# Four spots reordered in a two-layer float32 backbone: early partial sums, fold low parts on GpSimd, one weight split and one operand split moved

## The chip, the core and the metric

The kernel runs on one core of a Trainium2 chip. The metric is the device time of one execution in microseconds; the time of a kernel is the median of several runs. TensorE (PE) does the matmuls, VectorE (DVE), ScalarE (ACT) and GpSimd (POOL) do the elementwise work, and most DMAs are issued from the queue of SyncE (SP), a few from ACT's.

## What is computed

The reference runs two layers over 1024 latent tokens of width 1024 in float32, and a last RMSNorm. The even layer is a convolution branch and a bidirectional RG-LRU branch behind one input and one output projection; the odd layer is a pooling mixer. Cut to what the change touches:

```python
def even_mixer(h, h0, p):
    z = h @ p["w_in"]
    va, vg, ga, xb, gb = jnp.split(z, ...)
    y_a = conformer_conv(va, vg, p) * jax.nn.silu(ga)
    y_b, hT = rglru_branch(xb, p, h0, True)
    y_b = y_b * jax.nn.silu(gb)
    return jnp.concatenate([y_a, y_b], axis=-1) @ p["w_out"], hT

def odd_mixer(h, p, on_grid):
    u, g = jnp.split(h @ p["w_in"], [W_POOL], axis=-1)
    d = multiscale_pool(u) ...                       # four groups
    y = jnp.einsum("bngi,gij->bngj", d, p["w_grp"]) * p["scale"]
    return (y * jax.nn.silu(g)) @ p["w_out"]

for l in range(2):
    x = x + gate * mixer(modulate(rmsnorm(x)))
return rmsnorm(x, final_g)
```

## The kernel before

**Numbers in two parts.** A float32 matmul is done as three matmuls in a rounded format: every operand is split into a high part (a cast on ACT) and a low part (source minus high part, a subtraction, on DVE or POOL), and high by high, high by low and low by high are added up in PSUM. In names, `h` and `l` are the parts: `wh_gb` and `wl_gb` of a raw weight `wr_gb`, `y_b22h` and `y_b22l` of an operand. A low part needs its cast, and the cast needs the load.

**Quads.** The output projections of both layers, and more, work on quads: a 2 by 2 block product done as seven half-sized products by a Strassen-like scheme. The operand blocks are called `b11, t1, t2, b21, t3, b22, t4`; each product is 12 matmuls of 128x512. Three PSUM tiles, `qa`, `qc`, `qb`, hold the sums; `put` takes one out (DVE, `scalar_tensor_tensor`, PSUM times a gate plus what was there) before the next product that reuses or continues the tile may write it. A quad's weights are two loads `wr_...`, three sums of them, and seven splits into `wq_..._1` to `_7` (`wquad_steps`).

**Four places matter here**, in the order of the program.

- *gb products* (lines 1216 to 1250). The gate projection of the LRU branch, product by product of 48 matmuls, while DVE runs the convolution and `gated(n)` forms `sb = yr * sb`, its cast `ybh` (ACT) and its low part `ybl` (POOL); `yr` is loaded back from DRAM through a small ring of buffers. `gb_weights(j)` loads and splits the weight of product j: load on SP, cast `wh_gb` on ACT, low part `wl_gb` on POOL. `gb_silu(j)` reads product j out (`sb`, ACT). On ACT, POOL and DVE these steps run in the order in which the code is written (`act`, `cast`, `gp`, `vec` chain each instruction behind the one before on its engine). The weights `gb_weights(8)` and `(9)` are those of the next products, `wob`.
- *woa* (lines 1530 to 1600): the other half of the even layer's output projection, four quads of two row blocks each. `put` adds a product onto `x1`, which is first loaded from `x1_part` (the input plus the LRU half, stored at line 1260). The load sits in `put`, just ahead of the add, on SP. In the last quad `woa_ahead` also loads the four weights of fold 2 (`wr_wu_2_0` to `_3`), which the fold products after the last quad use; the low parts of the first two are made on DVE, those of the others on POOL. `square_acc` squares each finished block on ACT (`n1q`) and adds it up on DVE (`n1acc`).
- *wo1* (lines 1960 to 2035): the second part of the odd layer's output projection. Two quads are interleaved: `q0.b11, q0.t1, ..., q0.b21, q2.b11, q0.t3, q0.b22, q2.t1, q0.t4, ...`. Between `q0.b21` and `q2.b11` stands the block that loads operand t3, the weights of quad 2 (`wo1_weights(1, 2)`), the operands b22 and t4, and two blocks of `x2`.
- The operands of wo1 come from DRAM (`y_b22`, `y_t4`, two tiles of 128x1024 each) into rotating pools, b22 into one pool, t4 into another (`y_operands`, line 1790).

**What sets the order.** Within one engine the instructions run in program order. A scheduler writes that order when the kernel is built, from the code's order, the ties `issue_after` and `high_priority`, and the time at which it expects a tile's buffer to come free. So a step can end up elsewhere than where it is written.

Of the kernel before, what the change touches and what calls it, by code (L numbers as in the profile page):

```python
# [20 lines left out]
KT = D // P  # L21
H = 512
HALF = (slice(0, H), slice(H, S))
# [28 lines left out]
def body(ctx, tc, xT, ctxT, cc, ccol, modT, modW, win, gw, wout, wu, grp, wg, wo1, small, edge, ident, outT):  # L52
# [44 lines left out]
    def split(src, hi, lo, eng):  # L97
        return (nc.scalar.copy(hi, src),  # L98
                eng.tensor_tensor(out=lo, in0=src, in1=hi.bitcast(F32), op=sub))

    def held(after):
        return tc.issue_after(after.ins) if after is not None else nullcontext()
# [974 lines left out]
    def vtile(name):  # L1077
        return vpool.tile([P, H], F32, tag="v", name=name)
# [157 lines left out]
    gb_product(5, gws[5])  # L1236
    gated(1, 3)
    for j in range(3, KT + 1):
        if j == 4:
            gb_weights(j + 2)  # L1240
        if j < KT:
            gb_silu(j)
        if 4 < j < KT - 1:
            gb_weights(j + 2)
        if 3 < j < KT - 2:
            gb_product(j + 2, gws[j + 2])
        gated(j - 1, (0, 0, 4, 5, 5, 3, 1, 0)[j - 1])
        if j == KT:
            gb_weights(KT + 1)
            fill(8)  # L1250
        ln_sums()
# [239 lines left out]
    def quad_linked(w, name, ops, put, ahead, order, pend, other):  # L1491
# [35 lines left out]
                put(1, 0, b, None)  # L1527
        return nxt_, (last if len(order) == 2 else (lambda: run("t3"), last))

    def woa(m, w, ahead, pend):  # L1530
        for q in range(2):
            x1[m + q] = xtile(f"x1_{m + q}")

        def put(i, h, x, part):
            v, dr = x1[m + i][:, HALF[h]], x1_part[m + i][:, HALF[h]]
            if part != 1:
                nc.sync.dma_start(v, dr)
            nc.vector.scalar_tensor_tensor(out=v, in0=x, scalar=m0[:, 0, 2 * KT + m + i : 2 * KT + m + i + 1],
                                           in1=v, op0=mult, op1=add)
            if part != 0:  # L1540
                if m < KT - 4 or (m == KT - 4 and (i, h) == (0, 0)):
                    nc.sync.dma_start(dr, v)
                else:
                    late.append((dr, v))
                    if wlate:
                        late_stores()
                square_acc(nacc[h][:, :H], v, (m, i) == (0, 0), f"n1q{m}_{i}_{h}")
        return quad_linked(w, f"woa{m}", ya, put, ahead, {0: ("b22",), KT - 2: ("t3", "b22")}.get(m, ("b22", "t3")),
                           pend, m % 4 == 2)
# [10 lines left out]
    def w_raw(g, kp, out, eng=nc.gpsimd, low=None):  # L1560
        raw = wpool.tile([P, D], F32, tag="wr", name=f"wr_wu_{g}_{kp}")
        d = nc.sync.dma_start(raw, wu[g, kp])
        if out is None:
            hi, lo = [wpool.tile([P, D], F32R, tag=v, name=f"{v}_wu_{g}_{kp}") for v in ("wh", "wl")]
        else:
            hi, lo = [out(f"{v}_wu_{g}_{kp}", F32R) for v in ("wh", "wl")]
        split_held(raw, hi, lo, eng, low)
        return d, (hi, lo)

    def woa_ahead(m):  # L1570
        w = wo_weights(m + 2) if m < KT - 2 else None
        for _ in range((0, 4, 2, 0)[m // 2]):
            next(mods)
        if m == KT - 4:
            sel2.append(hpool.tile([P, H], F32R, tag="cH", name="sel2"))
            selector(sel2[0], nc.gpsimd)
        if m == KT - 2:
            with ExitStack() as octx:
                for v in parted:
                    octx.enter_context(tc.issue_after(v.ins))  # L1580
                g2.append(fold_in(2, d2tile, d2tile))
                octx.enter_context(tc.issue_after(graws[2].ins))
                for kp in range(2):
                    d, w_ = w_raw(2, kp, W2[kp], nc.vector)
                    w2.append(w_)
            wlate.append(d)
            late_stores()
        return w

    sel2 = []  # L1590
    last_ = None
    for m in range(0, KT, 2):
        w0, last_ = woa(m, w0, lambda: woa_ahead(m), last_)
    last_()
# [193 lines left out]
    def y_operands(part, raws, names=BOPS, alloc=None, later=None, hold=None):  # L1788
        for name in names:
            y_operand(yops[part], part, name, next(raws),  # L1790
                      alloc or (dtile if name in ("b11", "b21", "t4") else d2tile), later, hold)
# [11 lines left out]
    def wo1_weights(part, m, mid=None):  # L1803
        return wquad([wo1[m + i, part] for i in range(2)], f"wo{part}_{m}", wo1_ring,
                     part == 1 and m >= KT - 4, mid=mid)
# [204 lines left out]
    with tc.issue_after(q0.evac.ins):  # L2010
        late_ = []
        y_operands(1, iter([None]), BOPS[4:5])
        with held(y_loaded[0]):
            w = wo1_weights(1, 2)
        with tc.issue_after(loaded[0].ins):
            y_operands(1, iter([None] * 2), BOPS[5:], later=late_)
        for v in late_:
            split(*v, nc.vector)
        with held(y_loaded[1]):
            x2_load(2)  # L2020
# [313 lines left out]
```

## Time and profile before

| what | value |
|---|---|
| time, median of 3 runs | 1267.16 us (1267.01 to 1267.77) |
| span of the profiled execution, first to last instruction | 1263.6 us |
| outside the span, median less span | 3.56 us |
| granted TensorE clock, mean | 0.998 |
| busy: PE, DVE, ACT, POOL | 1249.8, 1139.3, 653.8, 295.7 us |

The profile is of one execution, and no time beside its span is recorded for it, so the median stands for its own time. PE is busy for 99% of the span. Timeline rows give the start and the length in us, the engine, the line, the operation with output and inputs, the count, and in brackets the idle time before it with what ended it. A matmul of 128x512 lasts 0.39 us, but the next starts 0.227 us after it, so gaps between starts show a wait. Line numbers are those of the kernel before; in the changed kernel they are 7 to 14 higher behind the second spot.

### The profile page before, as it was taken

How to read it: one execution, taken by the hardware profiler on the slowest of the kernel's cores; microseconds unless marked ns; L12 is line 12 of the kernel's file. 1: busy time of each engine (PE TensorE's matmuls, PEld its weight loads, DVE VectorE, ACT ScalarE, POOL GpSimd, SP SyncE). 2: the span in 40 equal slices, each digit the busy share in tenths (PEclk: the TensorE clock that was granted, in tenths of full speed). 3: DMA queues.
4: the chain of work that ended last, by engine and by line, in shares of the span. 5: the costliest groups of instructions: out<-in, count | busy, mean ns of one | idle time of the engine just before them, and what ended most of it. 6: DMA issues, size and time to landing. Idle time of an engine off the chain costs nothing.

```text
span 1263.6 us, 16209 instructions
## 1 busy us (share of the span) xinstructions
PE 1249.8 (99%) x5866; PEld 1035.6 (82%) x5866; DVE 1139.3 (90%) x1746; ACT 653.8 (52%) x952; POOL 295.7 (23%) x176
## 2 busy tenths in 40 slices
PE   9999999999999999999999999999999999999997
PEld 7788888888888888888887878888888888888786
DVE  7799999999999999998978969999899987977975
ACT  8464566656666534237535445744343444644642
POOL 0015364436444547543210023000000000000002
PEclk9999999999999999999999999999999999999999
DMA  9970121112121233442436666344323334759723
GB/s 376 388 254 33 52 65 46 63 43 75 42 84 42 84 119 132 159 150 84 147 112 225 202 206 183 103 136 148 125 94 140 117 125 126 268 199 335 285 71 134
DMA packets 78705, 182.29 MB, mean 144 GB/s; under 512 B 7712, under 2 KB 23328, under 8 KB 78624
## 3 DMA queue, kind: packets, MB, share of 16 engines
q1 hardware_dynamic: 67328, 172.33, 39.8%
q10 hardware_dynamic: 11296, 8.92, 2.2%
q8 instruction: 46, 0.75, 0.2%
q14 instruction: 35, 0.29, 0.1%
HBM read 137.18 MB, written 44.04 MB: 143 GB/s over the span
## 4 chain that ended last, share of the span: by engine, by line
PE 70%; DVE 18%; DMA 7%; issue 2%; ACT 2%; POOL 1%; SPq 0%; POOLq 0%; ACTq 0%; DVEq 0%
PE wob L670 7%; DVE conv L670 5%; PE va L670 5%; PE xb L670 4%; PE vg L670 4%; DVE l L670 3%; PE fold L670 3%; PE g L670 3%; PE qb_v L1153 2%; PE ga L670 2%; PE qb_g L1156 2%; PE ga L161 2%; PE qb_v L1156 2%; PE qb_g L1155 2%; PE qb_g L1153 2%
## 5 line engine op out<-in xcount | busy, mean ns | idle before, releaser
L670 DVE SCALAR_TENSOR_TENSOR conv<-u,sm,conv 128x505 f32<-128x505 f32 (+6 forms) x224 | 153.6, 744 | 1.0
L2045 POOL TENSOR_TENSOR o<-x,rr 128x256 f32<-128x256 f32 (+1 forms) x10 | 9.2, 952 | 448.4 <-ACT rr L2045 448.4
L670 ACT ACTIVATE l<-g,sm 128x512 f32<-128x512 f32 (+1 forms) x96 | 58.7, 619 | 57.7 <-PE g L670 57.0
L670 POOL TENSOR_TENSOR l<-l,l 128x1280 f32<-128x1280 f32 x16 | 47.1, 2967 | 25.6 <-ACT l L670 15.1
L670 PE MATMUL gb<-h0h,wl_gb 128*128 128x512 f32 x128 | 49.9, 390 | 0.4 <-POOL wl_gb L670 0.4
L670 PE MATMUL va<-h0h,wl_va 128*128 128x512 f32 x128 | 49.9, 390 | 0.2 <-DVE wl_va L670 0.2
L98 ACT CAST wq_g<-wr_g 128x512 fp32r<-128x512 f32 x48 | 28.2, 621 | 41.9 <-DMA wr_g<-wg 15.6
L670 PE MATMUL gb<-h0l,wh_gb 128*128 128x512 f32 x128 | 49.8, 389 | 0.0
L670 PE MATMUL gb<-h0h,wh_gb 128*128 128x512 f32 x128 | 49.8, 389 | 0.0
L670 PE MATMUL va<-h0l,wh_va 128*128 128x512 f32 x128 | 49.8, 389 | 0.0
L670 PE MATMUL va<-h0h,wh_va 128*128 128x512 f32 x128 | 49.8, 389 | 0.0
L670 PE MATMUL wob<-ybl,wh_wob 128*128 128x512 f32 x128 | 49.8, 389 | 0.0
L670 PE MATMUL wob<-ybh,wl_wob 128*128 128x512 f32 x128 | 49.8, 389 | 0.0
L670 PE MATMUL wob<-ybh,wh_wob 128*128 128x512 f32 x128 | 49.8, 389 | 0.0
L670 DVE TENSOR_TENSOR_SCAN l<-l,l 128x256 f32<-128x256 f32 (+1 forms) x32 | 48.7, 1521 | 1.1
L670 DVE SCALAR_TENSOR_TENSOR conv<-cL,wsum,conv 128x506 f32<-128x506 f32 (+3 forms) x70 | 48.1, 745 | 0.2
L670 POOL TENSOR_TENSOR l<-l,uc 128x1280 f32<-128x1280 f32 x16 | 47.6, 2999 | 0.0
L98 ACT CAST wq_wo<-wr_wo 128x512 fp32r<-128x512 f32 x48 | 28.6, 620 | 35.5 <-DVE wr_wo L1134 12.4
L98 ACT CAST wq_v<-wr_v 128x512 fp32r<-128x512 f32 x48 | 28.1, 620 | 33.7 <-DMA wr_v<-wfold 16.6
L670 PE MATMUL xb<-h0l,wh_xb 128*128 128x512 f32 x112 | 43.8, 391 | 0.0
L670 PE MATMUL xb<-h0h,wh_xb 128*128 128x512 f32 x112 | 43.8, 391 | 0.0
L670 POOL TENSOR_TENSOR wl_xb<-wr_xb,wh_xb 128x1024 fp32r<-128x1024 f32 x7 | 16.8, 2407 | 114.5 <-ACT wh_xb L670 114.5
(680 smaller groups left out, 4362.5 us busy)
## 6 DMA issues: line engine op xcount, KB each, us to landing
modw<-modW SPq DMA_DIRECT2D x16, 512.0 KB, 10.2
mod<-modT SPq DMA_DIRECT2D x32, 256.0 KB, 3.4
wr_v<-wfold SPq DMA_DIRECT2D x16, 512.0 KB, 4.0
wr_g<-wg SPq DMA_DIRECT2D x16, 512.0 KB, 4.3
wr_wo<-wo SPq DMA_DIRECT2D x16, 512.0 KB, 4.1
mod<-modT SPq DMA_DIRECT2D x14, 512.0 KB, 4.5
y_b<-y SPq DMA_DIRECT2D x24, 256.0 KB, 3.5
y_t<-y SPq DMA_DIRECT2D x24, 256.0 KB, 3.1
```

Of the source, the lines that this page charges most:

```text
L98: return (nc.scalar.copy(hi, src), eng.tensor_tensor(out=lo, in0=src, in1=hi.bitcast(F32), op=sub))
L161: mm(ps, hi[:, kc], xh[k][:, cols], start=(k == 0), stop=False)
L670: last[eng] = f(*args, **kw)
L1153: nc.tensor.matmul(ps, hi, xh[k], start=(first and k == 0), stop=False, skip_group_check=not first)
L1155: nc.tensor.matmul(ps, hi, xl[k], start=False, stop=False, skip_group_check=not first)
L1156: mm = nc.tensor.matmul(ps, lo, xh[k], start=False, stop=(k == KH - 1), skip_group_check=not first)
L2045: tail[eng] = f(*args, **kw)
```

## The change

1. In the loop over the gb products, `gb_weights(7)` (j = 5) moves ahead of `gb_silu(5)`.
2. For the first woa quad, the partial sums of blocks (1, second half) and (0, second half) are loaded ahead of the loop into small tiles `x1p`; `put` adds from there instead of from a load into `x1` just ahead of the add.
3. The low parts of the first two fold weights (`wl_wu_2_0`, `wl_wu_2_1`) are made on POOL instead of DVE.
4. In wo1, the loads of b22 and t4 and the split of b22 are passed into `wo1_weights(1, 2)` as its `mid`, which runs them after the weight's two loads, its first two splits and the sums; the split of t4 stays behind the weights.

```diff
--- before.py
+++ after.py
@@ -1236,11 +1236,11 @@
     gb_product(5, gws[5])
     gated(1, 3)
     for j in range(3, KT + 1):
-        if j == 4:
+        if 3 < j < KT - 2:
             gb_weights(j + 2)
         if j < KT:
             gb_silu(j)
-        if 4 < j < KT - 1:
+        if j == KT - 2:
             gb_weights(j + 2)
         if 3 < j < KT - 2:
             gb_product(j + 2, gws[j + 2])
@@ -1527,16 +1527,23 @@
                 put(1, 0, b, None)
         return nxt_, (last if len(order) == 2 else (lambda: run("t3"), last))
 
+    early = {}
+
+    def part_ahead(i, h):
+        early[i, h] = vtile(f"x1p_{i}_{h}")
+        nc.sync.dma_start(early[i, h], x1_part[i][:, HALF[h]])
+
     def woa(m, w, ahead, pend):
         for q in range(2):
             x1[m + q] = xtile(f"x1_{m + q}")
 
         def put(i, h, x, part):
             v, dr = x1[m + i][:, HALF[h]], x1_part[m + i][:, HALF[h]]
-            if part != 1:
+            base_ = early.pop((m + i, h), v) if part != 1 else v
+            if part != 1 and base_ is v:
                 nc.sync.dma_start(v, dr)
             nc.vector.scalar_tensor_tensor(out=v, in0=x, scalar=m0[:, 0, 2 * KT + m + i : 2 * KT + m + i + 1],
-                                           in1=v, op0=mult, op1=add)
+                                           in1=base_, op0=mult, op1=add)
             if part != 0:
                 if m < KT - 4 or (m == KT - 4 and (i, h) == (0, 0)):
                     nc.sync.dma_start(dr, v)
@@ -1581,7 +1588,7 @@
                 g2.append(fold_in(2, d2tile, d2tile))
                 octx.enter_context(tc.issue_after(graws[2].ins))
                 for kp in range(2):
-                    d, w_ = w_raw(2, kp, W2[kp], nc.vector)
+                    d, w_ = w_raw(2, kp, W2[kp], nc.gpsimd)
                     w2.append(w_)
             wlate.append(d)
             late_stores()
@@ -1589,6 +1596,8 @@
 
     sel2 = []
     last_ = None
+    part_ahead(1, 1)
+    part_ahead(0, 1)
     for m in range(0, KT, 2):
         w0, last_ = woa(m, w0, lambda: woa_ahead(m), last_)
     last_()
@@ -2010,11 +2019,16 @@
     with tc.issue_after(q0.evac.ins):
         late_ = []
         y_operands(1, iter([None]), BOPS[4:5])
+
+        def second_row():
+            with tc.issue_after(loaded[0].ins):
+                y_operands(1, iter([None] * 2), BOPS[5:], later=late_)
+            for v in late_[:2]:
+                split(*v, nc.vector)
+
         with held(y_loaded[0]):
-            w = wo1_weights(1, 2)
-        with tc.issue_after(loaded[0].ins):
-            y_operands(1, iter([None] * 2), BOPS[5:], later=late_)
-        for v in late_:
+            w = wo1_weights(1, 2, second_row)
+        for v in late_[2:]:
             split(*v, nc.vector)
         with held(y_loaded[1]):
             x2_load(2)
```

TensorE's order does not change. The order of the other engines at the places that matter:

SP's queue at spot 4, before: `wr_wo1_2` are the raw weights of quad 2, `y1_b22l` and `y1_t4l` the tiles into which the operands are loaded, `x2` the blocks that quad 2 adds onto.

```order
L1117 DMA wr_wo1_2_0_10063<-wo1 128x1024
L1117 DMA wr_wo1_2_1_10065<-wo1 128x1024
L1772 DMA y1_b22l0_10093<-y_b22_1_105 128x1024
L1772 DMA y1_b22l1_10096<-y_b22_1_105 128x1024
L1772 DMA y1_t4l0_10099<-y_t4_1_106 128x1024
L1772 DMA y1_t4l1_10102<-y_t4_1_106 128x1024
L1962 DMA x2_2_10113<-x1_part2_109 128x1024
L1962 DMA x2_3_10115<-x1_part3_110 128x1024
```

The same stretch of SP's queue now:

```order
L1117 DMA wr_wo1_2_0_10065<-wo1 128x1024
L1117 DMA wr_wo1_2_1_10067<-wo1 128x1024
L1781 DMA y1_t4l0_10085<-y_t4_1_106 128x1024
L1781 DMA y1_t4l1_10088<-y_t4_1_106 128x1024
L1971 DMA x2_2_10115<-x1_part2_109 128x1024
L1971 DMA x2_3_10117<-x1_part3_110 128x1024
L1781 DMA y1_b22l0_10079<-y_b22_1_105 128x1024
L1781 DMA y1_b22l1_10082<-y_b22_1_105 128x1024
```

The two loads of b22, which stood third and fourth, stand seventh and eighth, behind t4 and both blocks of `x2`.

ACT at spot 4, now: the casts of b22 are `y1_b22h0` and `y1_b22h1`. Before, the first stood ahead of `wq_wo1_2_6` and the second ahead of `wq_wo1_2_7`.

```order
L98 CAST wq_wo1_2_4_10108<-wr_wo1_2_1_10067 128x512
L98 CAST y1_t4h0_10087<-y1_t4l0_10085 128x1024
L98 CAST y1_t4h1_10090<-y1_t4l1_10088 128x1024
L98 CAST wq_wo1_2_7_10101<-ws_wo1_2_10072 128x512
L1467 ACTIVATE fin0_10052<-x2_0_9975 128x512
L2008 COPY qb_wo1_2_10121<-qac_wo1_2_0_10119 128x512
L98 CAST y1_b22h0_10081<-y1_b22l0_10079 128x1024
L1903 ACTIVATE x2_0_9975<-x2_0_9975,sm_115 128x512
L1914 COPY b_wo1_0_10146<-qb_wo1_0_9981 128x512
L98 CAST wq_wo1_2_3_10105<-wr_wo1_2_0_10065 128x512
L98 CAST y1_b22h1_10084<-y1_b22l1_10082 128x1024
```

Both casts of b22 now follow those of t4, and three instructions stand between the first and the second. On DVE the low parts moved in the same way: between the two of b22 stand an add into `x2_1` and the low part of `wq_wo1_2_3`.

DVE at spots 2 and 3. The place of spot 2 now: `ya_b22l` are the low parts of the first quad's operand b22, and the add takes `qc`'s first product out of PSUM.

```order
L99 TENSOR_TENSOR ya_t3l1_5650<-u3_2067,ya_t3h1_5648 128x512
L1545 SCALAR_TENSOR_TENSOR x1_1_5682<-qc_woa0_5684,m0_132,x1p_1_1_5677 128x512
L99 TENSOR_TENSOR ya_b22l0_5661<-u4_2402,ya_b22h0_5659 128x512
L99 TENSOR_TENSOR ya_b22l0_5661<-u5_2735,ya_b22h0_5659 128x512
L99 TENSOR_TENSOR ya_b22l1_5662<-u6_3069,ya_b22h1_5660 128x512
L99 TENSOR_TENSOR ya_b22l1_5662<-u7_3402,ya_b22h1_5660 128x512
L1134 TENSOR_TENSOR wr_woa2_1_5739<-wr_woa2_1_5739 128x512
```

The add stood behind the last row of this list; now it stands ahead of the four low parts.

The place of spot 3 on DVE now: `qb_woa6` and `qac_woa6_0` are PSUM tiles of the last quad.

```order
L107 TENSOR_TENSOR gl_2_1_6245<-graw_2_1_6242,gh_2_1_6244 128x1024
L1545 SCALAR_TENSOR_TENSOR x1_6_6161<-qb_woa6_6165,m0_132,x1_6_6161 128x512
L1471 TENSOR_TENSOR n1acc0_5675<-n1acc0_5675,n1q4_1_0_6207 128x512
L1545 SCALAR_TENSOR_TENSOR x1_6_6161<-qac_woa6_0_6163,m0_132,x1_6_6161 128x512
L1471 TENSOR_TENSOR n1acc0_5675<-n1acc0_5675,n1q6_0_0_6266 128x512
L1545 SCALAR_TENSOR_TENSOR x1_7_6162<-qb_woa6_6165,m0_132,x1_7_6162 128x512
L1471 TENSOR_TENSOR n1acc1_5676<-n1acc1_5676,n1q6_1_1_6283 128x512
```

Before, `wl_wu_2_0` stood ahead of the first add into `x1_6`, and `wl_wu_2_1` behind the add into `x1_7`; both are gone to POOL, which does nothing else there, and the first add has moved ahead of an `n1acc`. On ACT the cast `wh_wu_2_0` now stands ahead of the square `n1q4_1_0`, behind which it stood.

At spot 1, ACT casts `wh_gb7` ahead of the two `sb5` instead of behind them; POOL's order is as it was. On SP the load of `wr_wob1` stands ahead of the load of `yr5_0` instead of behind it, and the loads `x1p` of spot 2 stand each behind one of the two last stores of the partial sums (line 1260), ahead of the weight `wr_ga5`.

## Prediction

> **What bounds the kernel.** I read the page's busy times first, then the waits of PE, then the timeline around each wait, engine by engine.
>
> ```profile
> PE 1249.8 (99%) x5866; PEld 1035.6 (82%) x5866; DVE 1139.3 (90%) x1746; ACT 653.8 (52%) x952; POOL 295.7 (23%) x176
> ```
>
> PE is the bound: 1249.8 of 1263.6 us. Only what makes PE wait, or stop waiting, moves the time. PE's order doesn't change, so each spot is priced by the starts of its matmuls. PE's timeline, the row before and behind each wait that a spot is near:
>
> ```profile
> 478.82 0.39 PE L670 MATMUL gb<-h0h,wh_gb 128*128 128x512 f32 x1
> 479.05 0.39 PE L670 MATMUL gb<-h0l,wh_gb 128*128 128x512 f32 x1
> 479.89 0.50 PE L670 MATMUL gb<-h0h,wl_gb 128*128 128x512 f32 x1 [0.45 <-POOL wl_gb L670]
> ...
> 677.07 0.39 PE L1156 MATMUL qa_woa<-ya_b21h,wq_woa 128*128 128x512 f32 x1
> 678.23 0.47 PE L1153 MATMUL qc_woa<-ya_b22h,wq_woa 128*128 128x512 f32 x1 [0.77 <-ACT wq_woa L98]
> ...
> 735.20 0.39 PE L1156 MATMUL qac_woa<-ya_b21h,wq_woa 128*128 128x512 f32 x1
> 736.13 0.50 PE L1153 MATMUL qb_woa<-ya_t3h,wq_woa 128*128 128x512 f32 x1 [0.54 <-DVE x L1538]
> ...
> 1187.80 0.39 PE L1153 MATMUL qc_wo<-y_b22h,wq_wo 128*128 128x512 f32 x1
> 1189.16 0.39 PE L1153 MATMUL qc_wo<-y_b22h,wq_wo 128*128 128x512 f32 x1
> 1190.42 0.50 PE L1155 MATMUL qc_wo<-y_b22l,wq_wo 128*128 128x512 f32 x1 [0.87 <-DVE y_b22l L99]
> ```
>
> Undisturbed, a matmul starts 0.23 us after the one before (478.82 to 479.05). The four steps above are 0.84, 1.16, 0.93 and 1.26 us, so beyond 0.23 each they lose 0.61, 0.93, 0.70 and 1.03; the matmul behind each starts some 0.1 late as well, as the longer first one (0.50 for 0.39) tells. All four together are about 3.7 us, 0.3% of the time, and that is the most that the change can win.
>
> **Spot 1, the gate weight gb7 (about +0.7 us).** DVE and POOL around the wait, and the nearest rows of the same operations:
>
> ```profile
> 465.78 2.40 DVE L670 TENSOR_TENSOR sb<-yr,sb 128x512 f32<-128x512 f32 x1
> 471.82 0.68 DVE L670 TENSOR_TENSOR sb<-yr,sb 128x512 f32<-128x512 f32 x1
> 475.68 1.28 DVE L670 TENSOR_TENSOR lnsum<-lnsum,u 128x512 f32<-128x512 f32 x2
> ...
> 465.24 2.38 POOL L670 TENSOR_TENSOR wl_gb<-wr_gb,wh_gb 128x1024 fp32r<-128x1024 f32 x1
> 473.24 1.30 POOL L670 TENSOR_TENSOR ybl<-sb,ybh 128x512 fp32r<-128x512 f32 x1 [3.03 <-ACT ybh L670]
> 476.24 3.59 POOL L670 TENSOR_TENSOR wl_gb<-wr_gb,wh_gb 128x1024 fp32r<-128x1024 f32 x1 [1.70 <-ACT wh_gb L670]
> ```
>
> With its cast moved up, `wl_gb7` can follow the `ybl` that ends at 474.54, and take 2.38: done at 476.9, ahead of the matmul that waited until 479.89. That wait, 0.72 with its restart, is gone. But the same rows show that a DVE subtraction, sum or product of two SBUF tiles and a POOL one don't run together. The `sb` product takes 0.68 alone and 2.40 while `wl_gb` holds POOL from 465.24 to 467.62; and `wl_gb` takes 3.59 where DVE's `lnsum` came first. Moved up, `wl_gb7` comes first, and `lnsum`, due at 475.68, can't go on until 476.9. It ends near 477.5 (one takes about 0.6, the second a bit later) instead of 476.9, and the `sb` behind it in turn; by how much each step of this chain slips I put at 0.9, an estimate: the 1.2 that `lnsum` waits, less what later steps lost to `wl_gb` before and don't lose now. Here DVE's queue runs in written order and hardly idles, so the lateness travels along: `sb`, `ybh`, `ybl`, the buffers of `yr`, the next cast. Who waits for that are the wob products:
>
> ```profile
> 490.44 0.39 PE L670 MATMUL wob<-ybh,wh_wob 128*128 128x512 f32 x1
> ...
> 492.17 3.02 POOL L670 TENSOR_TENSOR ybl<-sb,ybh 128x512 fp32r<-128x512 f32 x2 [1.28 <-ACT ybh L670]
> 499.00 2.40 POOL L670 TENSOR_TENSOR wl_wob<-wr_wob,wh_wob 128x1024 fp32r<-128x1024 f32 x1
> ```
>
> `wob` reads operand block 6 with its 20th matmul, at 490.44 + 19 x 0.227 = 494.75; POOL has that low part, the first of the two at 492.17, by about 493.9: 0.8 early. The next product starts 48 matmuls after 490.44, at 501.3, and needs `wl_wob1` with its third matmul, 501.8; POOL has it at 501.4, 0.35 early. PE arrives 0.72 earlier than before and the chain comes 0.9 later, so the first misses by 0.8 (with the restart 0.9) and the second by what is left, 0.4 (0.5). Together 1.4 lost for 0.7 won: +0.7. If the chain doesn't slip, it still has only 0.35 to give: -0.35. If it follows PE, -0.7. If both slips are larger by half, +1.0.
>
> **Spot 2, the first woa quad (-1.0).** DVE, where the row at 674.33 is the four low parts of b22 and that at 677.34 the add that moves ahead of them:
>
> ```profile
> 674.33 2.49 DVE L99 TENSOR_TENSOR ya_b22l<-u,ya_b22h 128x512 fp32r<-128x512 f32 x4
> 677.34 0.74 DVE L1538 SCALAR_TENSOR_TENSOR x<-qc_woa,m,x 128x512 f32<-128x512 f32 x1
> ...
> 687.20 0.74 DVE L1538 SCALAR_TENSOR_TENSOR x<-qb_woa,m,x 128x512 f32<-128x512 f32 x1
> ```
>
> The wait list blames ACT for the 0.77, but the cast that it names isn't read then; what ends at 678.08 is the add that empties `qc`, which the matmul at 678.23 writes. Its product was two products, some 5.4 us, back, and the partial sum is now loaded a stage ahead. So the add runs from 674.33, and the first low part, needed by b22's second matmul at 677.5, is done by 675.8. PE goes on at 677.30: the whole 0.93 and the late restart, 1.0. Next to be late is the add at 687.20: it empties `qb` for t4, four products of 12 matmuls (10.9 us) behind 678.3, at 689.2 before and 688.2 now. DVE's queue is full up to there, so this add stays where it is and ends at 687.94, 0.2 early. I take the 1.0, and -0.6 as the other end, if DVE slips. The two loads on SP wait for the last stores and hold back `wr_ga5` behind them by under 1 us; no PE wait stands there to tell of it, so nothing.
>
> **Spot 3, the fold low parts (0).** DVE and ACT:
>
> ```profile
> 734.19 1.22 DVE L107 TENSOR_TENSOR wl_wu<-wr_wu,wh_wu 128x1024 fp32r<-128x1024 f32 x1 [1.51 <-ACT wh_wu L105]
> 735.34 0.74 DVE L1538 SCALAR_TENSOR_TENSOR x<-qb_woa,m,x 128x512 f32<-128x512 f32 x1
> 737.49 0.69 DVE L1471 TENSOR_TENSOR n1acc<-n1acc,n1q 128x512 f32<-128x512 f32 x1 [0.76 <-ACT n1q L1470]
> ...
> 733.11 1.05 ACT L105 CAST wh_wu<-wr_wu 128x1024 fp32r<-128x1024 f32 x1 [1.49 <-DMA wr_wu<-wu]
> ```
>
> DVE stood idle behind its place in the queue for the cast, and the add from `qb` behind it was late: 0.81. Without `wl_wu_2_0` that is gone. But on POOL it takes 2.4 (the 2.38 above) for DVE's 1.22, from 734.2 to 736.6, and shuts out the `n1acc` behind the square that ACT now makes after the cast, at 734.8. The add that empties `qac` follows at 737.3 to 738.0, just as b22 needs it (735.20 + 0.23 + 12 x 0.227 = 738.15). `wl_wu_2_1` does the same to the next `n1acc`, from about 737.4 to 739.8, and the add from `qb` behind that ends at 740.5 to 741.2 where t4 needs it at 740.87. I expect 0.4 to 0.9 back, and take 0 net; the ends are -0.8 (POOL disturbs nobody) and +0.4.
>
> **Spot 4, operands of wo1 (+4.3).** The order shows the reverse of what the code is written for: the two loads of b22 now stand behind t4 and `x2`. The last rows of the views of tiles `y_b22l` and `y_t4l` and of the line of the `x2` loads give the time from issue to landing, in that order, behind SP's rows; then ACT and DVE.
>
> ```profile
> 1175.21 1.43 SPq L1772 DMA_DIRECT2D y_b22l<-y_b  x2
> 1176.73 2.50 SPq L1772 DMA_DIRECT2D y_t4l<-y_t  x2
> 1180.17 1.57 SPq L1962 DMA_DIRECT2D x<-x_part  x2
> ...
> DMA to landing us min/median/max: 8.8/9.1/9.3
> ...
> DMA to landing us min/median/max: 9.6/9.9/10.3
> ...
> DMA to landing us min/median/max: 3.3/4.8/9.6
> ...
> 1184.37 1.05 ACT L98 CAST y_b22h<-y_b22l 128x1024 fp32r<-128x1024 f32 x1
> 1190.34 0.72 ACT L1894 ACTIVATE x<-x,sm 128x512 f32<-128x512 f32 x1
> 1191.89 0.58 ACT L1905 COPY b_wo<-qb_wo 128x512 f32<-128x512 f32 x1
> ...
> 1189.14 1.22 DVE L99 TENSOR_TENSOR y_b22l<-y_b22l,y_b22h 128x1024 fp32r<-128x1024 f32 x1
> ```
>
> The six loads land in the order of issue, at 1184.0, 1185.3 (1175.9 + 9.3), 1187.1, 1188.5, 1189.8 and 1191.0 (the second of the last pair is issued near 1181.4): about 1.4 us apart, 9 to 10 us after issue. So the queue is full, and the place in it sets the landing. As the last two, b22 lands near 1189.7 and 1191.0; that its loads were issued at 1175 before doesn't help. The first cast is done at 1190.8, the first low part at 1192.0 (1.22). The second cast stands behind the scaling, the copy and one more cast (0.72 and 0.58 in the rows, and some 0.6 for a cast half as wide as that of 1.05), and ends near 1193.4; its low part near 1194.6. The matmul that went on at 1190.42 goes on at 1194.7: +4.3. Nothing later takes it back, since PE is full again behind it. The lower end is +0.9: if the loads kept their landings, only the order on ACT and DVE would count, and the low part of the second tile would end near 1191.3. The upper end is 4.8, if one more instruction comes between.
>
> **The sum.** +0.7 - 1.0 + 0 + 4.3 = +4.0 us on the profiled execution's span of 1263.6, with the 3.56 between span and median: 1271.2, 0.3% slower. About 0.2%, 2.5 us, is what a measurement of this kernel tells from no change, so the bounds are 1264.6 and 1269.7.
>
> **The rivals.**
>
> *All four waits go and nothing takes their place*: -3.7, 1263.5. It needs b22 early in the queue, and POOL's work harmless; for it speaks only that each wait has its releaser named above. The new order of SP speaks against it. 0.08.
>
> *The loads land as before, or nearly*, and spot 4 costs 0.9: +0.6, 1267.8. The queue would have to have room; six landings 1.4 us apart speak against it. 0.13.
>
> *Spot 4 as forecast, but POOL's low parts cost DVE nothing that PE feels*: -0.35 - 1.0 - 0.8 + 4.3 = +2.2, 1269.3, just within no change. The slacks on which spots 1 and 3 hang are under 1 us, so this is near. 0.18.
>
> *The long wait halves PE's clock.* The windows behind the last matmuls, with the granted clock (PEclk) the figure before the last two:
>
> ```profile
> 1256.00:1257.00 1.00, 0.67 (x2) 0.30 (x2) 0.00 (x0) 0.21 (x1) 0.00 (x0) 1.00 1.03 346
> 1257.00:1258.00 1.00, 0.00 (x0) 0.00 (x0) 0.80 (x3) 0.16 (x1) 0.76 (x2) 0.68 0.41 139
> 1258.00:1259.00 1.00, 0.00 (x0) 0.00 (x0) 1.00 (x4) 0.00 (x0) 1.00 (x2) 0.50 0.00 0
> ```
>
> At the end of the kernel the clock falls to 0.50 within a second microsecond of rest. At spot 4 PE would find nothing to do from 1187.8 to 1190.8, and one matmul until 1192.0. If the clock falls there and takes as long as the wait, some 3 us, to come back, half of that is lost: 1.5 more, 1272.7. Its point is the arrival of b22: waits of about 1 us, as the four above, show a full clock. 0.25.
> By the Trainium skill, page "TensorE: Matmul & The Clock Gate", Part 1, the clock halves after an idle window of about 3.4 us and is full again after a busy one as long, which by that figure would be an estimate of 1.7 us instead of the 1.5; no run here shows yet a wait in mid-kernel that long.
>
> **How the numbers follow.** The forecast itself has 0.36. With the halved clock 0.61 lies above 1269.7, and a little more from the rival at 1269.3, less the forecast's own low end: slower 0.64. No change takes the two rivals at 1267.8 and 1269.3 and a part of that end: 0.27. Faster has 0.09. The range goes from 1266.5, which leaves out the case in which all waits go, to 1273.3, the halved clock with the upper ends of spot 4.
>
> **What would show it.** In the profile after: no step at 479 and 678, new steps near 494 and 502 with `ybl` or `wl_wob` as releaser; `n1acc` rows of 2 us or more near 735; b22 landing last of the six and a step of 3 to 4 us on `qc_wo` near 1188, released by ACT's or DVE's part of b22. It is wrong if b22 lands ahead of `x2` (then spot 4 costs little), or if the `sb` rows near 477 keep 0.68 and the wob products don't wait.

## The result and the profile after

The changed kernel takes 1275.42 us (median; 1273.52 to 1276.32) against 1267.16 (1267.01 to 1268.58) for the kernel before, measured beside it: a ratio of 1.0057, 95% interval 1.0043 to 1.0071, which is 5.4 to 9.0 us slower. The profiled execution took 1275.09 us for a span of 1273.3, at a mean granted clock of 0.995. The forecast, 1271.2, had the direction and most of the places; the size was too small. Of the runs further below, two of the ten with spot 4 alone took 3265.91 and 4498.40 us for a reason that nothing here shows; that kernel's ratio leaves them out, and its median is that of the other eight.

PE is still the bound. From the page of after, the busy times (before, PE had 1249.8):

```profile
PE 1255.0 (99%) x5866; PEld 1038.5 (82%) x5866; DVE 1140.8 (90%) x1744; ACT 654.1 (51%) x952; POOL 297.3 (23%) x178
```

With the same 5866 matmuls, PE is busy 5.2 us longer. It was given no more work, so some of its matmuls have become longer: a first hint of the clock. Three of the four waits of before are gone; the one for `y_b22l` is still there, with 1.2 for 0.9 and a longer one ahead of it. PE's timeline in after, at the four places in the order of the program (the old wait of spot 1, the new ones of spot 1, the old ones of spots 2 and 3, spot 4):

```profile
481.14 0.39 PE L670 MATMUL gb<-h0h,wl_gb 128*128 128x512 f32 x1
...
495.65 0.39 PE L670 MATMUL wob<-ybh,wh_wob 128*128 128x512 f32 x1
496.29 0.50 PE L670 MATMUL wob<-ybl,wh_wob 128*128 128x512 f32 x1 [0.25 <-POOL ybl L670]
...
502.32 0.39 PE L670 MATMUL wob<-ybh,wh_wob 128*128 128x512 f32 x1
503.05 0.50 PE L670 MATMUL wob<-ybl,wh_wob 128*128 128x512 f32 x1 [0.34 <-POOL ybl L670]
...
503.85 0.40 PE L670 MATMUL wob<-ybl,wh_wob 128*128 128x512 f32 x1
505.39 0.50 PE L670 MATMUL wob<-ybh,wl_wob 128*128 128x512 f32 x1 [1.14 <-POOL wl_wob L670]
...
681.04 0.39 PE L1153 MATMUL qc_woa<-ya_b22h,wq_woa 128*128 128x512 f32 x1
...
738.22 0.39 PE L1153 MATMUL qb_woa<-ya_t3h,wq_woa 128*128 128x512 f32 x1
...
1190.88 0.39 PE L1156 MATMUL qb_wo<-y_t3h,wq_wo 128*128 128x512 f32 x1
1194.40 0.49 PE L1153 MATMUL qc_wo<-y_b22h,wq_wo 128*128 128x512 f32 x1 [3.14 <-ACT y_b22h L98]
1196.09 0.79 PE L1155 MATMUL qc_wo<-y_b22l,wq_wo 128*128 128x512 f32 x1 [1.20 <-DVE y_b22l L99]
1196.69 0.63 PE L1156 MATMUL qc_wo<-y_b22h,wq_wo 128*128 128x512 f32 x1
```

The rows at 481.14, 681.04 and 738.22 stand where the steps were 0.84, 1.16 and 0.93 us; they have no idle time before them any more, and their steps are 0.22 or 0.23. New are 0.64, 0.73 and 1.54 in the `wob` products, and at spot 4 steps of 3.52 and 1.69 in place of 1.26. Behind the last, a matmul lasts 0.63 and more where it lasted 0.39. SP's queue at spot 4 in after, and then the last row of the view of tile `y_b22l`:

```profile
1178.67 1.01 SPq L1781 DMA_DIRECT2D y_t4l<-y_t  x2
1179.77 1.38 SPq L1971 DMA_DIRECT2D x<-x_part  x2
1182.14 1.87 SPq L1781 DMA_DIRECT2D y_b22l<-y_b  x2
```

```profile
DMA to landing us min/median/max: 10.1/10.2/10.4
```

The loads of b22 are issued last of the six and land 10 us later, behind the others.

**Where the time went.** All kernels here, but one that adds matmuls, issue the same 5866 matmuls in the same order, so the n-th matmul of one trace can be set against the n-th of another. The start of a matmul, less the start of the same one in before, grows or falls over each place by what the place costs. The columns are stretches in the time of before, in us; the executions are described under the experiments.

| profiled execution | up to 470 | spot 1, 470 to 510 | spot 2, 670 to 685 | 685 to 730 | spot 3, 730 to 745 | 745 to 1187 | spot 4, 1187 to 1205 |
|---|---|---|---|---|---|---|---|
| after | 1.87 | +1.88 | -1.01 | +0.05 | -0.83 | +1.35 | +6.39 |
| after, second profile | -0.11 | +0.35 | -1.01 | +0.03 | +0.75 | +3.57 | +6.27 |
| spot 1 alone | -0.17 | +1.89 | +0.04 | 0.00 | +0.80 | +0.39 | -0.01 |
| spot 2 alone | 0.05 | +0.69 | -1.01 | 0.00 | +2.18 | +2.55 | -0.11 |
| spot 3 alone | 0.02 | -0.06 | +0.02 | 0.00 | -0.83 | +1.57 | -0.01 |
| spot 4 alone | 0.13 | -0.32 | +0.04 | 0.00 | -0.53 | +0.71 | +4.83 |
| spot 4, b22 first | 0.25 | -0.33 | +0.03 | 0.00 | -0.83 | +3.23 | -0.13 |
| spot 1, low part in halves | 0.17 | +0.35 | +0.03 | +0.21 | +1.12 | +1.71 | +0.17 |
| spot 1, load order of before | 0.15 | +1.62 | +0.03 | 0.00 | +0.15 | +2.19 | +0.17 |
| spots 2 and 3 | 0.44 | +0.98 | -1.01 | +0.55 | +0.83 | +3.15 | +0.16 |
| spots 1, 2 and 3 | 1.01 | +1.42 | -1.01 | +0.69 | +0.78 | +1.71 | -0.02 |
| all four, b22 first | 0.30 | +0.32 | -1.01 | +0.03 | +0.56 | +2.21 | +0.21 |

The table also shows what a single profile can't tell. The stretch from 745 to 1187 holds no edit, yet it is 0.4 to 3.6 us longer in every other execution than in the one of before; spots 1 and 3 differ by 1.5 and 1.6 us between the two executions of the changed kernel. Most of what is left is spot 4.

### The profile page after: what moved, and what is told of

Same layout as the page of the kernel before. It is cut to its first block, busy times and chain, and to the rows that moved or that the text cites. A ratio compares the mean times of both kernels' runs of the same rounds, so it can differ in the third digit from the quotient of the medians.

```text
span 1273.3 us, 16211 instructions
## 1 busy us (share of the span) xinstructions
PE 1255.0 (99%) x5866; PEld 1038.5 (82%) x5866; DVE 1140.8 (90%) x1744; ACT 654.1 (51%) x952; POOL 297.3 (23%) x178
## 5 line engine op out<-in xcount | busy, mean ns | idle before, releaser
L670 PE MATMUL xb<-h0h,wl_xb 128*128 128x512 f32 x112 | 43.6, 389 | 0.0
```

Of the source, the lines that this page charges most:

```text
L670: last[eng] = f(*args, **kw)
```

## The experiments

The theory: the queue place of b22's loads makes a wait of some 4 us at spot 4, and spots 1 to 3 are near zero together. The rivals: the wait also halves PE's clock; the cost sits in spots 1 to 3 or in how the spots work on each other. Each ratio is to the kernel before, run beside it, with its 95% interval.

### The four spots one by one

Each kernel is the kernel before with one of the four edits; the diffs are the hunks of the change above. Spot 1 alone:

> Spot 1 alone. Theory from the two traces (POOL's low part shuts out DVE's lnsum, and the lateness grows along the ring of yr loads): the wait at 479 is gone (-0.7), three waits near 494 to 504 add 2.5, net +1.8 us. The prediction's own size: +0.7. If the waits at the wob products came from another spot: -0.7.

Spot 2 alone:

> Spot 2 alone. Theory: the wait at 677 is gone and nothing follows, -1.0 us. Rival: the new waits near 794 (+0.6) or 1115 (+0.7) of the changed kernel belong to the early loads, which shift tiles and later orders; then -1.0 plus one of these, between -0.4 and +0.3.

Spot 3 alone:

> Spot 3 alone. Theory from the trace of the changed kernel: the wait at 735 is gone and nothing takes its place, -0.8 us. The prediction: 0, with n1acc rows of 2 us or more and a new wait before t4 near 741. Rival: the new wait near 794 belongs to this spot, then -0.2.

Spot 4 alone:

> Spot 4 alone. Theory: b22 loaded last gives 3.6 us of wait and a halved clock for about 6 us gives 3.0 more, +6.6 us. The prediction's own size: +4.3 without the clock, +5.8 with it. Rival: the loads' place does not matter and only the order on ACT and DVE does, +0.9.

| kernel | median us | ratio, 95% interval |
|---|---|---|
| spot 1 | 1268.71 | 1.0011 (1.0000 to 1.0021) |
| spot 2 | 1269.65 | 1.0016 (1.0004 to 1.0028) |
| spot 3 | 1268.49 | 1.0009 (0.9998 to 1.0020) |
| spot 4 (eight runs) | 1272.57 | 1.0042 (1.0028 to 1.0057) |

Spot 4 holds 5 of the 7 us. Each of the others is within 0.2% of before, and spot 2, which removes 1.0 us in each of its executions in the table, did not show as faster (its interval even lies just above 1): its profile has 2.2 us at the fold weight's load and 2.6 behind, in places that it doesn't touch (the first is explained below). Over all sessions the kernel before itself ran from 1264.3 to 1274.1 us.

PE's timeline with spot 4 alone:

```profile
1187.61 0.39 PE L1156 MATMUL qb_wo<-y_t3h,wq_wo 128*128 128x512 f32 x1
1190.63 0.50 PE L1153 MATMUL qc_wo<-y_b22h,wq_wo 128*128 128x512 f32 x1 [2.64 <-ACT y_b22h L98]
1192.32 0.61 PE L1155 MATMUL qc_wo<-y_b22l,wq_wo 128*128 128x512 f32 x1 [1.19 <-DVE y_b22l L99]
```

The places are those of the forecast (first cast done at 1190.8, first low part at 1192.0). But the 0.61 of the last row is a matmul on a slower clock, as in after. This profiled execution, 1270.79 us, is the quickest of the eight. What holds up the casts of b22 stands on ACT, whose rows up to the first of them are these, then DVE's low part of the second tile:

```profile
1183.84 2.34 ACT L98 CAST wq_wo<-wr_wo 128x512 fp32r<-128x512 f32 x4 [3.35 <-DVE wr_wo L1134]
1186.09 1.99 ACT L98 CAST y_t4h<-y_t4l 128x1024 fp32r<-128x1024 f32 x2
1187.99 0.61 ACT L98 CAST wq_wo<-ws_wo 128x512 fp32r<-128x512 f32 x1
1188.50 0.62 ACT L1467 ACTIVATE fin<-x 128x512 f32<-128x512 f32 x1
1189.03 0.57 ACT L1999 COPY qb_wo<-qac_wo 128x512 f32<-128x512 f32 x1
1189.55 1.03 ACT L98 CAST y_b22h<-y_b22l 128x1024 fp32r<-128x1024 f32 x1
...
1193.45 1.22 DVE L99 TENSOR_TENSOR y_b22l<-y_b22l,y_b22h 128x1024 fp32r<-128x1024 f32 x1
```

ACT has no idle time from 1183.84 to the cast at 1189.55, and t4 had landed at 1185.05, before its casts. b22's first tile landed at 1189.50. So ACT's order alone, with b22 behind t4 and three other steps, would have put the cast where it is, even if b22 had landed sooner. In after the cast starts 0.8 us after the landing, in its second profile within 0.1. The second low part is done at 1194.67, where the forecast has 1194.6.

### Spot 4 with the loads of b22 tied ahead

The two loads of b22 are tied to be issued ahead of those of t4 and `x2`; the code of the casts and low parts stays where the change puts it. `y_last` is the last load that `y_operands` issued; the lines that set it are left out here.

```diff
             with tc.issue_after(loaded[0].ins):
-                y_operands(1, iter([None] * 2), BOPS[5:], later=late_)
+                y_operands(1, iter([None]), BOPS[5:6], later=late_)
+            with tc.issue_after(y_last[0].ins):
+                y_operands(1, iter([None]), BOPS[6:], later=late_)
```

> Spot 4 with the two loads of b22 tied ahead of t4's and x2's, as in the kernel before. Theory (the place in the queue is the cost): b22 lands near 1184 and 1185.3, no wait of 3 us, no halved clock: the 4.8 to 6.4 us of spot 4 are gone, and the old wait of 1.0 may shrink; -1.0 to 0 against before. Rival (the new order on ACT and DVE or the split in mid-weight is the cost): still +0.9 or more.

1268.29 us, ratio 1.0009 (0.9999 to 1.0018). The whole cost of spot 4 is gone. What is left is the old wait: its place costs 0.13 less than before, so the edit as intended wins about nothing there, since the second cast and low part of b22 are hardly earlier. The last row of the view of tile `y_b22l` in this kernel, where spot 4 alone has 10.9/11.0/11.1, then two rows of ACT:

```profile
DMA to landing us min/median/max: 7.8/8.1/8.5
...
1186.60 1.05 ACT L98 CAST y_b22h<-y_b22l 128x1024 fp32r<-128x1024 f32 x1
...
1190.58 1.05 ACT L98 CAST y_t4h<-y_t4l 128x1024 fp32r<-128x1024 f32 x1
```

With the loads, the scheduler has put the casts of b22 back ahead of those of t4. So the cost lies in the order that it wrote for b22, loads and casts together. No kernel here moves one without the other; by ACT's rows above, the order of the casts is enough for the wait with spot 4 alone.

### Spot 4 with PE kept busy through the wait

Twelve matmuls into an unused half of a PSUM tile stand ahead of b22's first matmul, and five each ahead of its first and third matmul that need a low part. Their sums are used by nothing. The kernel writes the product of b22 out; cut to the added calls:

```diff
+    busy(12)
     for k in range(KH):
         step(ps, hi, xh[k], start=False, stop=False)
+        if k in (0, 2):
+            busy(5)
         step(ps, hi, xl[k], start=False, stop=False)
         step(ps, lo, xh[k], start=False, stop=(k == KH - 1))
```

> Spot 4 alone, but PE repeats matmuls into an unused bank while b22 is missing (12 ahead of the product, 5 behind its first and 5 behind its seventh matmul); the result is not changed by them. Theory (wait and clock are two costs): the granted clock stays 1.00, the product of b22 ends when its data allow, 4.3 us later than before, against 4.8 (and 6.4 in the changed kernel's trace) with the halved clock; so 0.5 to 2 us faster than spot 4 alone. Rival (the clock record is a symptom and costs nothing): same as spot 4 alone, or slower by the extra matmuls.

1272.17 us, ratio 1.0035 (1.0021 to 1.0048). The windows over the place, with the granted clock before the last two figures:

```profile
1190.00:1194.00 4.00, 3.82 (x17) 2.72 (x15) 4.00 (x6) 4.00 (x7) 0.00 (x0) 1.00 0.72 242
1194.00:1198.00 4.00, 3.47 (x16) 2.69 (x15) 2.52 (x3) 2.33 (x4) 0.00 (x0) 1.00 0.00 0
```

The clock stays at 1.00, so the halving does come from PE's rest. The time itself, 1272.17 against 1272.57 for spot 4 alone, is too close to tell a gain; 0.5 to 2 us were expected.

What the wait costs without the clock is read from the last input that PE waits for, the low part of b22's second tile, which the eighth of the 12 matmuls reads. Here and in after it is made in these rows of DVE:

```profile
1195.31 1.21 DVE L99 TENSOR_TENSOR y_b22l<-y_b22l,y_b22h 128x1024 fp32r<-128x1024 f32 x1
```

```profile
1197.22 1.22 DVE L99 TENSOR_TENSOR y_b22l<-y_b22l,y_b22h 128x1024 fp32r<-128x1024 f32 x1
```

From the start of the last matmul of `q0.t3` to its end it is 2.79 us in before (1187.57 to 1190.36), 7.06 with spot 4 alone (1187.61 to 1194.67), 7.22 here (1189.30 to 1196.52, with one weight cast and one low part fewer between b22's two), 7.56 in after (1190.88 to 1198.44) and 7.70 in its second profile (1191.14 to 1198.84). Less the 2.79, the wait costs 4.3, 4.4, 4.8 and 4.9. In the nine executions of the table whose clock doesn't fall here, the same difference agrees with the column of spot 4 within 0.03, and in after neither DVE nor ACT has idle time on the way to that low part, so it doesn't hang on PE's clock. What the table has beyond it is the clock: 0.6 with spot 4 alone (4.83 less 4.27), 1.6 in after (6.39 less 4.77) and 1.4 in its second profile (6.27 less 4.91). The half clock itself slows more than that, but part of it runs while PE would wait for this low part anyway.

### Why the clock cost more in after than with spot 4 alone

The windows of spot 4 alone, then of after, cut at the edges of the clock (the first figure behind the length is the time in which PE had work):

```profile
1185.74:1189.16 3.42, 2.26 (x10) 1.52 (x9) 3.42 (x6) 3.42 (x6) 0.00 (x0) 1.00 1.04 419
1189.16:1192.57 3.41, 0.75 (x2) 0.44 (x3) 3.41 (x5) 3.41 (x6) 0.00 (x0) 1.00 0.45 181
1192.57:1195.98 3.41, 3.41 (x9) 2.44 (x9) 3.30 (x5) 2.87 (x5) 0.00 (x0) 0.50 0.35 94
```

```profile
1191.58:1194.99 3.41, 0.49 (x1) 0.19 (x1) 3.41 (x5) 3.41 (x7) 0.00 (x0) 1.00 0.81 306
1194.99:1198.41 3.42, 2.32 (x6) 1.82 (x6) 3.42 (x5) 3.42 (x6) 0.00 (x0) 0.50 0.09 11
1198.41:1201.82 3.41, 3.41 (x10) 2.61 (x9) 1.66 (x4) 1.41 (x3) 0.00 (x0) 0.50 0.40 143
```

The clock stands still within a window of 3.41 us and changes at its end. A window in which PE had work for 0.49 or 0.75 us ends with the half clock; a window that PE fills ends with the full one. In after the first window on the half clock began with the rest of the wait for the low part, and the 2.32 us of work in it were not enough: a second half-clock window followed; in the second profile of after it was so with 2.55 us. With spot 4 alone the first window on the half clock was full of work, and there was no second. That the windows run on a fixed grid shows at the end of the kernel, where the clock falls again. Windows of 0.1 us around the edges, in after:

```profile
1194.90:1195.00 0.10, 0.00 (x0) 0.00 (x0) 0.10 (x2) 0.10 (x2) 0.00 (x0) 0.96 0.00 0
1201.80:1201.90 0.10, 0.10 (x2) 0.09 (x1) 0.10 (x1) 0.00 (x0) 0.00 (x0) 0.91 0.00 0
1266.60:1266.70 0.10, 0.00 (x0) 0.00 (x0) 0.00 (x0) 0.10 (x1) 0.00 (x0) 0.86 1.08 369
```

A mean of 0.96 says that the fall lies 92% into its window, at 1194.992. So the edges of after are 1194.992, 1201.818 and 1266.672, apart by 6.826 (two times 3.413) and 71.680 (21 times 3.413) from the first; those with spot 4 alone, read in the same way, are 1192.568, 1195.982 and 1260.836, apart by 3.414 and 68.268 (20 times 3.413). The Trainium skill, page "TensorE: Matmul & The Clock Gate", Part 1, states a free-running window of 3413 ns, a half clock after an idle one and a full clock after a busy one; these edges agree, and add that a window with work for 2.32 of 3.41 us doesn't bring the full clock back. A window with as little, 2.26 us, did not take it away either (the first row with spot 4 alone).

### Spots 2 and 3; spots 1, 2 and 3; all four with b22 first; the changed kernel again

The first two are the hunks of those spots, the third the change with the tie for b22's loads as above, the last the changed kernel without an edit.

> Spots 2 and 3 alone: the waits at 677 (1.0) and 735 (0.8, or whatever the landing of the fold weight makes of it) should both be gone at once, and nothing new stand in their place. The local prices say -1.8 us, ratio 0.9986, faster than both kernels. The rival, that whatever these spots win is given back to later load landings (spot 2 alone read 1.0016, with waits that its edit doesn't touch), says 1.000 or above, with new waits near 735 or 795 that belong to the edit because they come back.

> The change without spot 4. If the cost sits in spot 4 as read from the trace (6.4 to 6.6 us locally), this kernel is the kernel before plus 1.8 - 1.0 - 0.8 = 0.0 us: ratio 1.000, and 0.9986 where the low part ybl6_0 loses or wins the race for the lock in such a way that spot 1 costs only 0.4. The rival, that the four spots work on each other and the 7.2 us are not a sum, says 1.002 or above.

> All four spots, with the two loads of b22 tied ahead of those of t4 and x2. The clock should stay at 1.00 near 1190, b22 land near 1186 and 1187, and the time fall back to that of the change without spot 4 (1.000, at most 0.3 us from it), so 6 to 7 us below the changed kernel. If spot 4 costs something besides the place in the queue, it lies above the other by more than 1 us.

> The changed kernel once more, unedited, for a second execution. The step at qc_wo should again be 2.8 to 3.3 and 1.5 us. If the length of the halved clock is a matter of the execution, it may be 3.4 us here as with spot 4 alone (local cost of spot 4 then 4.8) or 6.8 as in the first profile (6.5); if spots 1 to 3 make it longer, it is 6.8 again. The third wait at wob (1.3 to 1.4) comes only if POOL's ybl of block 6 starts ahead of DVE's sb of block 6.

| kernel | median us | ratio, 95% interval |
|---|---|---|
| spots 2 and 3 | 1267.40 | 0.9997 (0.9986 to 1.0009) |
| spots 1, 2 and 3 | 1268.94 | 1.0009 (0.9999 to 1.0019) |
| all four, b22 first | 1268.66 | 1.0003 (0.9989 to 1.0018) |
| changed kernel again | 1275.20 | 1.0057 (1.0041 to 1.0073) |

With b22's loads first, the change costs nothing that can be measured, and 6.5 us (1275.20 less 1268.66) are gone: the four spots add up, and the order of b22 in spot 4 is the loss. The second profile of after repeats the steps at spot 4 (its first wait is 3.4) and the double clock window. No version beats before; spots 2 and 3 come nearest, 1.2 us short by the medians of the -1.8 that their waits promised, which is the edge of their interval. Their timelines show how it can be lost; the profiled execution, 1271.01 us, is the slowest of the twelve.

**Spot 3 gives the wait back.** POOL, DVE and PE with spots 2 and 3:

```profile
736.81 2.40 POOL L107 TENSOR_TENSOR wl_wu<-wr_wu,wh_wu 128x1024 fp32r<-128x1024 f32 x1 [9.15 <-ACT wh_wu L105]
739.38 2.64 POOL L107 TENSOR_TENSOR wl_wu<-wr_wu,wh_wu 128x1024 fp32r<-128x1024 f32 x1 [0.17 <-PE qb_woa L1156]
...
737.24 2.52 DVE L1471 TENSOR_TENSOR n1acc<-n1acc,n1q 128x512 f32<-128x512 f32 x1 [2.60 <-ACT n1q L1470]
741.18 1.40 DVE L1471 TENSOR_TENSOR n1acc<-n1acc,n1q 128x512 f32<-128x512 f32 x1 [0.76 <-ACT n1q L1470]
742.50 0.74 DVE L1545 SCALAR_TENSOR_TENSOR x<-qb_woa,m,x 128x512 f32<-128x512 f32 x1
...
743.29 0.50 PE L1153 MATMUL qb_woa<-ya_t4h,wq_woa 128*128 128x512 f32 x1 [1.33 <-DVE x L1545]
```

Each `wl_wu` on POOL stretches the `n1acc` that falls into it, from 0.69 to 2.52 and 1.40, and the add from `qb` behind the second is late for t4. This is the chain that the forecast describes, with 1.5 us back instead of 0.4 to 0.9. In the first profile of after and with spot 3 alone it didn't happen. Counted with PE's matmul at 735.20 in before as the mark, the first fold weight landed there at 732.4 and 732.7 instead of 734.0 to 734.6 as in the other four, so that the second `n1acc` was over before the second `wl_wu` began. The six executions with spot 3 cost -0.83 twice and +0.56 to +0.83 four times; the seven others, of the table and of before, lie at the same place between -0.83 and +2.18, as the load of the fold weight lands sooner or later (0 at 733.0, +0.80 at 733.8, +1.12 at 734.1, +2.18 at 735.2). The means are +0.2 and +0.4: no gain to speak of. At a late landing spot 3 does help: 734.6 costs +0.8 with it, where the series without it would give about +1.6, an estimate.

**Spot 2 may give its win back at that load.** From issue to landing the first fold weight took 5.9 to 8.3 us (mean 7.2) in the six executions with spot 2, and 4.6 to 7.1 (mean 6.0) in the eight without it. PE comes 1.0 us sooner, and the load seems not to. With this spread that is suggested and not shown.

### Spot 1: why its cost is 0.3 or 1.9

Two kernels with spot 1 alone and one more edit. In the first, POOL makes the low part of gb7 in two halves, so that DVE's `lnsum` may get between them; in the second, the load of `wr_wob1` is tied behind that of `yr5_0`, where it stood before.

```diff
-        gp(out=lo, in0=raw, in1=hi.bitcast(F32), op=sub)
+        for c in (HALF if name == "gb7" else [slice(0, D)]):
+            gp(out=lo[:, c], in0=raw[:, c], in1=hi[:, c].bitcast(F32), op=sub)
```

```diff
-            gb_weights(KT + 1)
+            with tc.issue_after(yr_load[5, 0].ins):
+                gb_weights(KT + 1)
```

> Spot 1 with the low part of gb7 made in two halves of 128x512 on POOL. Theory (one POOL instruction shuts DVE's two-source operation out for its whole length): lnsum starts after the first half, its pair takes about 1.5 instead of 2.4, the chain slips by 0.3 to 0.6 instead of 1.2, and the waits at 494 to 504 fall from 2.4 to under 1.2; net between -0.3 and +0.6. Rival (the order of the loads on SP makes the lateness): still +1.7.

> Spot 1 with the load of wr_wob1 tied behind that of yr5_0, as before. Theory (POOL shuts DVE out): lnsum still takes 2.4 and the waits at 494 to 504 stay within 0.4 of the 2.4 of spot 1 alone, net +1.3 to +1.9. Rival (SP's order): the waits shrink below 1, net -0.7 to 0.

Ratios 1.0011 (0.9998 to 1.0025) and 1.0004 (0.9994 to 1.0013). The halves missed their aim: the pair of `lnsum` still takes 2.38, and the `sb` behind it starts at 477.83 against 477.79 with spot 1 alone. The first of the pair did get in between the halves, but the second half on POOL, from 475.59, then held up the second of the pair:

```profile
475.53 0.68 DVE L670 TENSOR_TENSOR lnsum<-lnsum,u 128x512 f32<-128x512 f32 x1
476.13 1.78 DVE L670 TENSOR_TENSOR lnsum<-lnsum,u 128x512 f32<-128x512 f32 x1
```

The load order isn't the cause either, for with it the place costs 1.62. Yet the first of the two cost 0.35. What differs is one pair of instructions, `sb` of block 6 on DVE and a `ybl` on POOL. POOL and DVE in after, then in its second profile:

```profile
494.95 1.29 POOL L670 TENSOR_TENSOR ybl<-sb,ybh 128x512 fp32r<-128x512 f32 x1 [1.28 <-ACT ybh L670]
502.96 2.38 POOL L670 TENSOR_TENSOR wl_wob<-wr_wob,wh_wob 128x1024 fp32r<-128x1024 f32 x1
...
495.13 1.65 DVE L670 TENSOR_TENSOR sb<-yr,sb 128x512 f32<-128x512 f32 x1 [0.26 <-DMA yr<-yb_raw]
```

```profile
492.60 3.05 POOL L670 TENSOR_TENSOR ybl<-sb,ybh 128x512 fp32r<-128x512 f32 x2 [1.28 <-ACT ybh L670]
499.43 2.40 POOL L670 TENSOR_TENSOR wl_wob<-wr_wob,wh_wob 128x1024 fp32r<-128x1024 f32 x1
...
492.55 0.69 DVE L670 TENSOR_TENSOR sb<-yr,sb 128x512 f32<-128x512 f32 x1
```

Where POOL starts first, `sb` takes 1.65 for 0.69, the chain behind it slips, and `wl_wob` is made at 502.96 instead of 499.43. Of this 2.0 us are the lag of the whole trace (1.87 and -0.11 at 470 in the table), and 1.5 are the slip; PE's step there is 1.54. Where DVE starts 0.05 us ahead, that step is 0.46. In the seven executions with spot 1, POOL was first in four (cost 1.42 to 1.89) and DVE in three (0.32 to 0.35). Without spot 1, POOL was first with spot 2 alone and with spots 2 and 3 (0.69 and 0.98); with the kernel before, spot 3 alone and the kernels with spot 4 alone it was DVE (-0.33 to 0). At the same outcome spot 1 thus costs about 0.9 with POOL first and 0.5 with DVE first. So spot 1 doesn't create the race, which is open in the kernel before as well; `sb` starts when its load lands, and a start 0.02 to 0.2 us behind POOL's decides it. That the race makes the third wait is read from the traces alone; no kernel here forced its outcome.

## Why the prediction was right or wrong, point by point

- **The bound and the four old waits**: right. PE's order and count are the same, and three of the four waits are gone, the fourth replaced.
- **Spot 1, +0.7**: the mechanism is right, the size is a mean of two cases. The two waits that it names came, by `ybl` and by `wl_wob`, and with POOL first one more by `ybl`; `sb` behind `lnsum` kept its 0.68. The seven executions have a mean of +1.12, those without spot 1 in the table and before +0.16, so about +1.0. The prediction took each slip as a fixed 0.9; the runs show a race that decides between 0.3 and 1.9, and with the race left aside 0.5 or 0.9.
- **Spot 2, -1.0**: right, -1.01 in all six executions. Its other end, -0.6, was touched where DVE slipped: +0.55 and +0.69 came back by 730 in two of them.
- **Spot 3, 0**: right, with both its ends seen, -0.83 and +0.83, and the chain through `n1acc` as described. In the profile of after alone it would look wrong: the `n1acc` row of 2.52 is there, but costs PE nothing.
- **Spot 4, the wait of +4.3**: right with spot 4 alone, 4.3, by the cast and the low part that the prediction names; in the two profiles of after it was 4.8 and 4.9. b22 lands last of the six, as forecast, and back in front in the queue it lands 8 instead of 11 us after issue. But that its landing sets the time of the first cast came out by coincidence: ACT's order holds the cast up as long or longer. So the lower end was wrong: with the landings of before, the order on ACT and DVE would not have cost 0.9 but, by ACT's rows, at least as much as the forecast; no kernel here tried it. The rival at 1267.8, which rests on this 0.9, had its price wrong too.
- **The halved clock, a rival at 0.25, +1.5**: here the prediction failed. It was to be part of the sum. The prediction took 1 us waits as evidence of a full clock through a rest of 3 us, one matmul and another 1.2 us. The runs show the clock halved in all three executions in which PE rested through such a wait, and that PE's single matmul between (0.49 us of a window of 3.41) doesn't keep it up. Its price in the changed kernel, 1.6 and 1.4, is near the 1.5, but that is luck: the half clock lasted not some 3 us but 6.8, two windows, and much of it ran while PE would have waited for the second low part anyway.
- **The sum.** With the terms as measured, +1.0 - 0.8 - 0.2 + 6.3 is +6.3 us (the -0.8 is the -1.01 less a mean of 0.2 given back by 730; the 6.3 is spot 4 with the clock), inside the measured 5.4 to 9.0. Of the 2.3 that the forecast lacks beside its +4.0, the clock is 1.5, the longer wait 0.5 and spot 1 0.3. The sum gives 1273.5; the rest up to 1275.42 is in none of the four places and stays open. In the other sessions the kernel before had medians of 1267.81 to 1268.03 instead of 1267.16, which would account for less than half of it.
- **The 3.56 us between span and median**: in every execution with both numbers the time is 1.8 us above the span, so the profiled execution of before was itself about 1.8 us quicker than the median. The table shows where, for the most part: in the stretch from 745 to 1187. The sum against the median was right all the same, as the change has no part in that.

## What to carry to other kernels

Before code is moved that issues loads, look at where the loads end up in a queue that is full, and where the casts that wait for them end up on their engine: the scheduler moved both here, and by ACT's rows the place of the casts alone was enough for the wait. Price a PE rest of several microseconds with the clock in it. Here, after a window of 3.4 us with little work, at least one more ran at half speed, and a wait that reached into that one added another; what PE would wait for anyway behind the rest comes off the price. And where two engines shut each other out, an edit that moves one of them by a tenth of a microsecond decides a microsecond, differently from run to run: one profile is not enough to price it.

## What the runs showed of the hardware that was not expected

- The clock falls and rises on a fixed grid of 3.413 us (edges above), and a window with PE busy for two thirds changes it neither way: full stayed full with 2.26 us of work, half stayed half with 2.32 and 2.55.
- A subtraction split in two on POOL let one DVE instruction in between and no more: the first `lnsum` took 0.68 us, the second 1.78 beside the second half, and the pair 2.38 us beside one piece or two.
- Executions of one unchanged kernel differ by up to 9 us (1265.26 to 1274.05), and part of it comes through load landings that sit at the edge of a wait: the same place cost -0.83 to +2.18 us in the kernels with the same code at it.
